# Differential attention: one VectorE combination per query tile, copies and epsilon term on ScalarE, third buffers for queries and gates

## The chip, the core and the metric

The kernel runs on one core of a Trainium2 chip. The metric is the device time of one execution in microseconds. The engines are TensorE (PE in the rows; PEld is its weight load), VectorE (DVE), ScalarE (ACT), GpSimd (POOL) and SyncE (SP), whose queue issues most of the transfers; a name with q at its end (SPq, ACTq) is an engine's own queue of issues and semaphore waits. Each engine works through its instructions in order.

## The reference

The reference is one step of a two-layer hybrid backbone. It is run for 1024 latent tokens and 128 context tokens, width 1024. In each layer an input projection feeds three groups of heads (differential attention, gated DeltaNet, mLSTM); their outputs go through one output projection, and a SwiGLU feed-forward follows. The change touches the attention and, by one buffer, the merging of the two other groups. Cut to these, with names shortened:

```python
# differential attention: 4 heads, two maps m of 64 columns each, values of 128 columns
s = einsum('bqhmd,bkhmd->bhmqk', q, k) * 64 ** -0.5
p = softmax(s, axis=-1)
w = p[:, :, 0] - lam * p[:, :, 1]
a_out = einsum('bhqk,bkhe->bqhe', w, v)
a = rms_norm(a_out, attn_g) * (1 - lam_init)          # over the 128 columns, EPS = 1e-6
# the other two groups
d = rms_norm(o_delta, delta_g) * silu(bg)
m = sigmoid(co) * rms_norm(h_m, mlstm_g)
out = concatenate([a, d, m], -1) @ w_out
```

A latent query reads 1024 latent keys and 128 cached context keys; a context query reads the 128 context keys alone.

## The kernel before

The whole program is unrolled. Everything is float32; matrix products of the projections are made of three passes over a high and a low part (`mm3`). For each layer the order in the source is: `begin` and `w_in` (projections, gates, chunk matrices, inverses), `mixers` (scan, attention, second half of the output projection), the first half of the output projection, the feed-forward.

In `mixers` the scan over chunks (`delta_step`, `mlstm_step`, `merge`) is written first, then the loads of `x`, then the attention, then `w_out`. But the framework is told `schedule_with_timeline_sim=True`: a planner simulates the program with costs of its own and writes the order of each engine's queue. The trace shows attention's instructions between those of the last inverses (`prep2`) and of the scan; in layer 0 they run from 545 to 906 us, in layer 1 from about 2375 to 2757 us. In layer 1 the end of attention runs beside the output projection.

`attention` takes a head at a time, and in it blocks of 256 queries: four latent ones and one of 128 context queries. A block loads its queries (tile `Q`, two buffers, four transfers on the sync queue, line 1235). Then, for each tile of 128 queries (`j`), so 32 latent and 4 context tiles a layer:

1. For both maps, scores of 9 key blocks in three groups of 384 columns (line 1250, PSUM tile `s`, two buffers). VectorE scales each group into `e` (four buffers) and takes the maximum (line 1251); line 1253 takes the maximum of the three; ScalarE makes the exponentials of all 1152 columns in one instruction, with their sum (line 1256).
2. `rz` is the factor of the second map, -lam times the ratio of the sums (lines 1260 and 1261). The weights are not divided by the sum; the norm that follows takes it out again.
3. The combination `e0 + rz * e1`: for groups 0 and 1 (`DVG`) one VectorE instruction each (line 1266), for group 2 two GpSimd instructions (lines 1268 and 1269).
4. Transposes of the combined weights by TensorE, a group into one PSUM tile `t` (one buffer, line 1277), and a copy into `wt` (line 1280): groups 0 and 1 on ScalarE, group 2 (`DVT`) on VectorE. In context tiles the single group 0 goes by the first of each choice.
5. The product with the values (line 1284, PSUM tile `o`). ScalarE squares and sums it (line 1287). VectorE makes the epsilon term, EPS times the square of the first map's sum (line 1289), and adds the mean square (line 1290). GpSimd raises it to the power -0.5 (line 1291), ScalarE scales the product by it (line 1292).

After a block, `out` transposes its tiles (line 1215), scales them (line 1217) and stores them to `CAT` (line 1218). `tail` and `TAIL` could put this off by a block; `TAIL` is False, so they do nothing.

`merge` loads a chunk's gates (tile `bc`, two buffers, line 1184), norms the chunk's rows of the two other groups, multiplies with the gates, transposes and stores to `CAT` (line 1205). Its gate tile is written in place (line 1196) and read last by GpSimd (line 1197).

The names `DVG`, `DVT` and `TAIL` are constants: `(0, 1)`, `(2,)` and `False`.

Of the kernel before, what the change touches and what calls it, by code (L numbers as in the profile page):

```python
# [10 lines left out]
F32R = mybir.dt.float32r  # L11
AF = mybir.ActivationFunctionType
ALU = mybir.AluOpType
# [4 lines left out]
P = 128  # L18
# [12 lines left out]
NCH = 9  # L31
CVW = 1160
CVO = 1156
DVG = (0, 1)
DVT = (2,)
TAIL = False
WTB = 6
PLO = ()
PST = (1, 3, 5, 6)
# [31 lines left out]
class Kern:  # L71
# [1108 lines left out]
    def merge(self, l, c):  # L1180

        nc, S, sc, pz = self.nc, self.S, self.sc, self.pz
        bc = self.t(sc, [P, 512], "bc", 2)
        nc.sync.dma_start(bc, S["BC"][c])
        th = self.t(sc, [P, 512], "bh", 2)
        nc.scalar.activation(th, bc, AF.Tanh, scale=0.5)
        hv = lambda a: a.rearrange("p (h v) -> p h v", v=64)
        src = self.OH[:, c, :]
        r = self.t(sc, [P, 512], "m2", MB)
        nc.scalar.activation(r, src, AF.Square)  # L1190
        ms = self.t(sc, [P, 8], "ms", 2)
        nc.vector.reduce_sum(ms, hv(r), axis=AX.X)
        nc.vector.scalar_tensor_tensor(out=ms, in0=ms, scalar=1.0 / 64, in1=self.me[:, c].rearrange("p a h -> p (a h)"), op0=ALU.mult, op1=ALU.add)
        nc.gpsimd.tensor_tensor(out=ms, in0=ms, in1=self.mhalf[:, :8], op=ALU.pow)
        nc.gpsimd.tensor_tensor(out=hv(r), in0=hv(src), in1=ms[:, :, None].to_broadcast([P, 8, 64]), op=ALU.mult)
        nc.vector.scalar_tensor_tensor(out=bc[:, 0:256], in0=th[:, 0:256], scalar=1.0, in1=bc[:, 0:256], op0=ALU.add, op1=ALU.mult)
        nc.gpsimd.tensor_tensor(out=r[:, 0:256], in0=r[:, 0:256], in1=bc[:, 0:256], op=ALU.mult)
        nc.vector.scalar_tensor_tensor(out=r[:, 256:512], in0=th[:, 256:512], scalar=1.0, in1=r[:, 256:512], op0=ALU.add, op1=ALU.mult)
        pt = self.ps(pz, "z", 2)
        for p in range(4):  # L1200
            nc.tensor.transpose(pt[:, 128 * p:128 * p + 128], r[:, 128 * p:128 * p + 128], self.ident)
        ct = self.t(sc, [P, 4, 128], "m2", MB)
        for i in range(2):
            nc.scalar.activation(ct[:, 2 * i:2 * i + 2], pt[:, 256 * i:256 * i + 256].rearrange("p (a t) -> p a t", a=2), AF.Copy, scale=self.hg[l][:, i:i + 1])
        nc.sync.dma_start(S["CAT"][4:8, :, 128 * c:128 * c + 128].rearrange("a p t -> p a t"), ct)

    def attention(self, l):

        nc, S, at, pa = self.nc, self.S, self.at, self.pa
        tail = []  # L1210

        def out(fin, h, q0, nq):
            pf = self.ps(pa, "o", 2)
# [5 lines left out]
        for h in range(H):  # L1219
            K = []  # L1220
            for m in range(2):
                k = self.t(at, [P, NT + P], "K", 3, F32R)
                r = 64 * (h % 2) + 32 * m
                for lk in range(2):
                    nc.sync.dma_start(k[64 * lk:64 * lk + 64].bitcast(F32), S["KD"][h // 2, lk, r:r + 32].rearrange("r p t -> (r p) t"))
                K.append(k)
            V = self.t(at, [P, 10, 128], "V", 2)
            nc.sync.dma_start(V, S["VD"][:, :, 128 * h:128 * h + 128].rearrange("s p e -> p s e"))
            r0 = 64 * (h % 2)
            for q0 in range(0, NT, 256):  # L1230
                nq = min(256, NT - q0)
                q = self.t(at, [P, 2, 2, 256], "Q", 2, F32R)
                for hh in range(2):
                    for hl in range(2):
                        nc.sync.dma_start(q[64 * hh:64 * hh + 64, :, hl, :nq].bitcast(F32),
                                     S["QD"][h // 2, hl, r0:r0 + 64, :, q0:q0 + nq].rearrange("(m r) p t -> (r p) m t", m=2))
                ctx = q0 >= NL
                kt = [9] if ctx else list(range(9))
                groups = [kt] if ctx else [kt[0:3], kt[3:6], kt[6:9]]
                fin = self.t(at, [P, 256], "fin", 2)  # L1240
                for j in range(nq // 128):
                    es, zs = [], []
                    for m in range(2):
                        e = self.t(at, [P, NT], "e", 4)
                        mx = self.t(at, [P, 4], "mx", 4)
                        for i, ks in enumerate(groups):
                            w = 128 * len(ks)
                            p = self.ps(pa, "s", 2)
                            for hl in range(2):
                                nc.tensor.matmul(p[:, :w], lhsT=q[:, m, hl, 128 * j:128 * j + 128], rhs=K[m][:, 128 * ks[0]:128 * ks[0] + w], start=hl == 0, stop=hl == 1)  # L1250
                            nc.vector.tensor_scalar(out=e[:, GW * i:GW * i + w], in0=p[:, :w], scalar1=0.125, scalar2=None, op0=ALU.mult, op1=ALU.max, accum_out=mx[:, i:i + 1])  # L1251
                        nm = self.t(at, [P, 1], "nm", 4)
                        nc.vector.tensor_reduce(out=nm, in_=mx[:, :len(groups)], axis=AX.X, op=ALU.max, negate=True)
                        z = self.t(at, [P, 1], "zs", 8)
                        ev = e[:, :128 * len(kt)]
                        nc.scalar.activation(ev, ev, AF.Exp, bias=nm, accum_out=z)
                        es.append(e)
                        zs.append(z)
                    rz = self.t(at, [P, 1], "rz", 4)
                    nc.vector.reciprocal(rz, zs[1])  # L1260
                    nc.vector.scalar_tensor_tensor(out=rz, in0=rz, scalar=self.nlam, in1=zs[0], op0=ALU.mult, op1=ALU.mult)
                    for i, ks in enumerate(groups):
                        cs = slice(GW * i, GW * i + 128 * len(ks))
                        w0, w1 = es[0][:, cs], es[1][:, cs]
                        if i in DVG:
                            nc.vector.scalar_tensor_tensor(out=w0, in0=w1, scalar=rz, in1=w0, op0=ALU.mult, op1=ALU.add)
                            continue
                        nc.gpsimd.tensor_scalar(out=w1, in0=w1, scalar1=rz, scalar2=1.0, op0=ALU.mult, op1=ALU.mult)
                        nc.gpsimd.tensor_tensor(out=w0, in0=w0, in1=w1, op=ALU.add)
                    if tail and TAIL:  # L1270
                        out(*tail.pop())
                    WT = []
                    for i, ks in enumerate(groups):
                        n = len(ks)
                        p = self.ps(pa, "t", 1)
                        for a in range(n):
                            nc.tensor.transpose(p[:, 128 * a:128 * a + 128], es[0][:, GW * i + 128 * a:GW * i + 128 * a + 128], self.ident)
                        pv = p[:, :128 * n].rearrange("p (a t) -> p a t", a=n)
                        WT.append(self.t(at, [P, 3, 128], "wt", WTB))
                        (nc.vector.tensor_copy if i in DVT else nc.scalar.copy)(WT[i][:, :n], pv)  # L1280
                    po = self.ps(pa, "o", 2)[:, :128]
                    for i, ks in enumerate(groups):
                        for a, kx in enumerate(ks):
                            nc.tensor.matmul(po, lhsT=WT[i][:, a], rhs=V[:, kx, :], start=kx == kt[0], stop=kx == kt[-1])  # L1284
                    sq = self.t(at, [P, 128], "sq", 2)
                    ms = self.t(at, [P, 1], "ams", 4)
                    nc.scalar.activation(sq, po, AF.Square, accum_out=ms)
                    z2 = self.t(at, [P, 1], "z2", 4)
                    nc.vector.scalar_tensor_tensor(out=z2, in0=zs[0], scalar=EPS, in1=zs[0], op0=ALU.mult, op1=ALU.mult)
                    nc.vector.scalar_tensor_tensor(out=z2, in0=ms, scalar=1.0 / 128, in1=z2, op0=ALU.mult, op1=ALU.add)  # L1290
                    nc.gpsimd.tensor_tensor(out=z2, in0=z2, in1=self.mhalf[:, 0:1], op=ALU.pow)
                    nc.scalar.activation(fin[:, 128 * j:128 * j + 128], po, AF.Copy, scale=z2)
                tail.append((fin, h, q0, nq))
                if not TAIL:
                    out(*tail.pop())
                yield
        if tail:
            out(*tail.pop())


    def w_out(self, l, x, half, pool, tags, psp, bufs, raw):
# [252 lines left out]
```

## Time and profile before

| | |
|---|---|
| runs of the kernel before, median of 3 | 3688.73 us (3680.83 to 3689.36) |
| the profiled execution | 3690.29 us, span 3688.5 us |
| TensorE matmuls | 3517.3 us busy, 95% of the span, 22770 instructions |
| TensorE weight loads | 3345.0 us, 91% |
| VectorE | 2296.8 us, 62%, 5361 instructions |
| ScalarE | 1133.3 us, 31% |
| GpSimd | 662.7 us, 18% |
| mean granted TensorE clock | 0.969 of full speed |

How to read it: times come from one profiled execution; an engine is busy while an instruction runs on it. Matmuls are pipelined and their ends are modelled, so a busy TensorE isn't one at its peak. Shares over the span mix stages with different limits, so the rows below are for stretches. A group of instructions has a line of the kernel, an engine, an operation, the tile written and those read, shapes and a count, and then busy us, the mean ns of one, and the idle time just before them with what ended it. A wait is put down to the release that came last.

### The profile page before, as it was taken

What the parts mean: (1) busy time and instruction counts of PE and PEld (TensorE: products, weight loads), DVE (VectorE), ACT (ScalarE), POOL (GpSimd) and SP (SyncE); (2) the same over time, 40 slices, a digit from 0 to 9 for tenths busy, and PEclk for the clock granted to TensorE, in tenths of its full rate; (3) what the DMA queues carried; (4) which work ended last, traced back from release to release, by engine and by line L of the source; (5) the groups of instructions that cost most, each with busy time, mean ns of one, the idle gap of its engine ahead of it and who ended that gap; (6) DMA issues with size and microseconds to landing.
All of it is one profiled execution on the core that took longest, in us unless ns stands there. A gap on an engine that the chain in (4) does not pass through costs nothing.

```text
span 3688.5 us, 59491 instructions
## 1 busy us (share of the span) xinstructions
PE 3517.3 (95%) x22770; PEld 3345.0 (91%) x22770; DVE 2296.8 (62%) x5361; ACT 1133.3 (31%) x2383; POOL 662.7 (18%) x903
## 2 busy tenths in 40 slices
PE   7999989987999999999999998999899999999998
PEld 6998888986999999999989888888788999999997
DVE  7797778887465556654486478578867243333335
ACT  6324325455241111111143341344545111111111
POOL 2014322474110000000020243035612000000001
PEclk8999988999999999999999999899999999999999
DMA  5477643864222222221132672578341111111111
GB/s 209 137 243 263 222 114 118 269 186 146 66 66 81 78 83 86 97 71 49 56 118 88 223 265 93 143 218 230 106 134 47 41 42 48 43 41 41 46 46 58
DMA packets 279011, 434.14 MB, mean 118 GB/s; under 512 B 26568, under 2 KB 188424, under 8 KB 278472
## 3 DMA queue, kind: packets, MB, share of 16 engines
q1 hardware_dynamic: 249496, 324.30, 27.6%
q10 hardware_dynamic: 29232, 106.05, 8.9%
q8 instruction: 180, 2.95, 0.3%
q14 instruction: 103, 0.84, 0.1%
HBM read 315.85 MB, written 114.39 MB: 117 GB/s over the span
## 4 chain that ended last, share of the span: by engine, by line
PE 78%; DVE 10%; DMA 5%; issue 3%; ACT 2%; POOL 1%; SPq 1%; ACTq 0%; POOLq 0%; DVEq 0%
PE pd L189 7%; PE pd L190 6%; PE pd L191 6%; PE pg L191 5%; PE pu L190 5%; PE pu L191 5%; PE pu L189 5%; PE pg L190 5%; PE pg L189 5%; PE dn L189 5%; PE dn L190 5%; PE dn L191 5%; PE s L1250 3%; PE o L1284 2%; DMA Q<-QD 1%
## 5 line engine op out<-in xcount | busy, mean ns | idle before, releaser
L362 DVE SCALAR_TENSOR_TENSOR x<-pd,mod,x 128x256 f32<-128x256 f32 (+1 forms) x832 | 404.8, 514 | 597.2 <-PE pd L191 596.0
L183 ACT CAST wh<-wr 128x1024 fp32r<-128x1024 f32 (+1 forms) x219 | 229.1, 1047 | 877.7 <-PE pu L190 462.1
L184 DVE TENSOR_TENSOR wl<-wr,wh 128x1024 fp32r<-128x1024 f32 (+1 forms) x219 | 268.7, 1233 | 169.7 <-ACT wh L183 169.2
L299 POOL TENSOR_TENSOR nacc<-nacc,nsq 128x384 f32<-128x384 f32 x48 | 51.8, 1080 | 1755.4 <-issue 1572.5
L189 PE MATMUL pd<-hh,wh 128*128 128x384 f32 x1056 | 359.4, 340 | 7.3 <-DVE x L362 5.1
L189 PE MATMUL pg<-uh,wh 128*128 128x384 f32 x1056 | 357.4, 338 | 2.6 <-ACT uh L342 2.6
L190 PE MATMUL pg<-ul,wh 128*128 128x384 f32 x1056 | 357.8, 339 | 1.0 <-DVE ul L347 1.0
L189 PE MATMUL pu<-uh,wh 128*128 128x384 f32 x1056 | 355.7, 337 | 0.0
L190 PE MATMUL pu<-ul,wh 128*128 128x384 f32 x1056 | 355.5, 337 | 0.0
L190 PE MATMUL pd<-hl,wh 128*128 128x384 f32 x1056 | 355.5, 337 | 0.0
L191 PE MATMUL pg<-uh,wl 128*128 128x384 f32 x1056 | 354.6, 339 | 0.0
L191 PE MATMUL pd<-hh,wl 128*128 128x384 f32 x1056 | 354.4, 337 | 0.0
L191 PE MATMUL pu<-uh,wl 128*128 128x384 f32 x1056 | 350.4, 336 | 0.0
L189 PE MATMUL dn<-uh,wh 128*128 128x384 f32 x864 | 296.6, 343 | 5.7 <-ACT gw L952 4.4
L190 PE MATMUL dn<-ul,wh 128*128 128x384 f32 x864 | 295.9, 342 | 0.0
L191 PE MATMUL dn<-uh,wl 128*128 128x384 f32 x864 | 295.5, 342 | 0.1
L1250 PE MATMUL s<-K,Q 128*128 128x384 f32 (+1 forms) x800 | 223.6, 388 | 30.9 <-DVE e L1251 18.1
L1251 DVE TENSOR_SCALAR_CACHE_REDUCE e<-s 128x384 f32<-128x384 f32 (+1 forms) x400 | 208.9, 540 | 33.6 <-PE s L1250 27.1
L189 PEld LDWEIGHTS pd<-hh,wh 128*128 128x128 f32 x1056 | 198.8, 188 | 18.6 <-issue 7.7
L189 PEld LDWEIGHTS pg<-uh,wh 128*128 128x128 f32 x1056 | 199.6, 189 | 4.5 <-ACT uh L342 2.8
L385 DVE TENSOR_TENSOR hs<-pu,hs 128x384 f32<-128x384 f32 x132 | 73.1, 554 | 208.5 <-PE pu L191 201.7
L191 PEld LDWEIGHTS pg<-uh,wl 128*128 128x128 f32 x1056 | 199.1, 189 | 3.8
(354 smaller groups left out, 8233.1 us busy)
## 6 DMA issues: line engine op xcount, KB each, us to landing
wr<-in_w_gu_dram ACTq DMA_DIRECT2D x88, 512.0 KB
aw<-in_w_mod_dram SPq DMA_DIRECT2D x96, 256.0 KB
wr<-in_w_dn_dram ACTq DMA_DIRECT2D x44, 512.0 KB
wr<-in_w_st_dram ACTq DMA_DIRECT2D x36, 512.0 KB
rd<-RD SPq DMA_DIRECT2D x36, 512.0 KB
aw<-in_w_mod_dram SPq DMA_DIRECT2D x32, 512.0 KB
Q<-QD SPq DMA_DIRECT2D x128, 128.0 KB
RM<-em SPq DMA_DIRECT2D x36, 384.0 KB
```

What stands on the lines that cost most here:

```text
L183: nc.scalar.copy(hi, r)
L184: (eng or nc.vector).tensor_tensor(out=lo, in0=r, in1=hi.bitcast(F32), op=ALU.subtract)
L189: mm(out, lhsT=wh, rhs=xh, start=start, stop=False)
L190: mm(out, lhsT=wh, rhs=xl, start=False, stop=False)
L191: mm(out, lhsT=wl, rhs=xh, start=False, stop=stop)
L299: (nc.gpsimd if k in PST else nc.vector).tensor_tensor(out=self.acc[g], in0=self.acc[g], in1=s, op=ALU.add)
L362: nc.vector.scalar_tensor_tensor(out=x[g][k][:, lo:hi], in0=ps[:, lo:hi], scalar=gate[:, k, cnd:cnd + 1], in1=x[g][k][:, lo:hi], op0=ALU.m ...
L385: nc.vector.tensor_mul(s, pu[:, :GW], s)
L1250: nc.tensor.matmul(p[:, :w], lhsT=q[:, m, hl, 128 * j:128 * j + 128], rhs=K[m][:, 128 * ks[0]:128 * ks[0] + w], start=hl == 0, stop=hl == 1)
L1251: nc.vector.tensor_scalar(out=e[:, GW * i:GW * i + w], in0=p[:, :w], scalar1=0.125, scalar2=None, op0=ALU.mult, op1=ALU.max, accum_out=mx[ ...
L1284: nc.tensor.matmul(po, lhsT=WT[i][:, a], rhs=V[:, kx, :], start=kx == kt[0], stop=kx == kt[-1])
```

## The change

In each latent query tile, the combination becomes one VectorE instruction over all 1152 columns; the two GpSimd instructions go. All copies out of the `t` tile are on ScalarE. The epsilon term is made by two ScalarE activations: a square with the scale sqrt(EPS), and an identity with the scale 1/128 and the first as its bias. The tile `Q` gets a third buffer, and so does `merge`'s tile `bc`. The constants and the unused `tail` go with them. In context tiles (128 columns) the combination stays what it was.

```diff
-        bc = self.t(sc, [P, 512], "bc", 2)
+        bc = self.t(sc, [P, 512], "bc", 3)
...
-                q = self.t(at, [P, 2, 2, 256], "Q", 2, F32R)
+                q = self.t(at, [P, 2, 2, 256], "Q", 3, F32R)
...
-                    for i, ks in enumerate(groups):
-                        cs = slice(GW * i, GW * i + 128 * len(ks))
-                        w0, w1 = es[0][:, cs], es[1][:, cs]
-                        if i in DVG:
-                            nc.vector.scalar_tensor_tensor(out=w0, in0=w1, scalar=rz, in1=w0, op0=ALU.mult, op1=ALU.add)
-                            continue
-                        nc.gpsimd.tensor_scalar(out=w1, in0=w1, scalar1=rz, scalar2=1.0, op0=ALU.mult, op1=ALU.mult)
-                        nc.gpsimd.tensor_tensor(out=w0, in0=w0, in1=w1, op=ALU.add)
-                    if tail and TAIL:
-                        out(*tail.pop())
+                    w0, w1 = [e[:, :128 * len(kt)] for e in es]
+                    nc.vector.scalar_tensor_tensor(out=w0, in0=w1, scalar=rz, in1=w0, op0=ALU.mult, op1=ALU.add)
...
-                        (nc.vector.tensor_copy if i in DVT else nc.scalar.copy)(WT[i][:, :n], pv)
+                        nc.scalar.copy(WT[i][:, :n], pv)
...
-                    nc.vector.scalar_tensor_tensor(out=z2, in0=zs[0], scalar=EPS, in1=zs[0], op0=ALU.mult, op1=ALU.mult)
-                    nc.vector.scalar_tensor_tensor(out=z2, in0=ms, scalar=1.0 / 128, in1=z2, op0=ALU.mult, op1=ALU.add)
+                    nc.scalar.activation(z2, zs[0], AF.Square, scale=math.sqrt(EPS))
+                    nc.scalar.activation(z2, ms, AF.Identity, scale=1.0 / 128, bias=z2)
...
-                tail.append((fin, h, q0, nq))
-                if not TAIL:
-                    out(*tail.pop())
+                out(fin, h, q0, nq)
```

## Rows read from the trace of the kernel before

**Rows 1.** busy time by stretch: us of each engine in brackets' order, granted clock, DMA

```profile
545.00:905.00 360.00, 328.62 (x2734) 294.06 (x2735) 296.63 (x990) 195.26 (x470) 169.99 (x211) 0.94 0.62 185
2375.00:2760.00 385.00, 354.11 (x2615) 325.96 (x2613) 305.40 (x986) 190.63 (x446) 167.64 (x212) 0.94 0.59 172
1200.00:1400.00 200.00, 199.90 (x1145) 197.61 (x1144) 119.72 (x261) 30.77 (x47) 0.00 (x0) 1.00 0.25 82
```

**Rows 2.** waits of TensorE, 545 to 905 us: total us, times, longest

```profile
PE s L1250 <- DVE e L1251: 7.8, 15, 1.1
PE t L1277 <- ACT wt L1280: 6.6, 9, 2.7
PE s L1250 <- DMA Q<-QD: 5.1, 4, 1.9
PE o L1284 <- DVE wt L1280: 4.5, 6, 1.3
```

**Rows 3.** the same, 2375 to 2760 us

```profile
PE s L1250 <- DVE e L1251: 10.3, 17, 1.5
PE s L1250 <- DMA Q<-QD: 5.0, 2, 3.1
PE o L1284 <- DVE wt L1280: 3.1, 3, 2.2
```

**Rows 4.** groups by line and shape, ScalarE, whole span

```profile
L1256 ACT ACTIVATE e<-e,nm 128x1152 f32<-128x1152 f32 x128 | 161.0, 1257 | 88.8 <-DVE nm L1253 85.0 <-DVE z L1290 2.5 <-DVE den L1171 0.5
L1280 ACT COPY wt<-t 128x384 f32<-128x384 f32 x128 | 60.7, 474 | 31.4 <-PE t L1277 31.2
L861 ACT COPY X<-Nd 32x128 f32<-32x128 f32 x136 | 40.2, 295 | 81.4 <-DMA RD<-X 50.8 <-DVE Nd L839 29.0
L154 ACT ACTIVATE ea<-par 128x8 f32<-128x8 f32 x2 | 0.3, 200 | 0.0
```

**Rows 5.** score matmuls: their group, 545 to 905 us; their line, whole span

```profile
L1250 PE MATMUL s<-K,Q 128*128 128x384 f32 (+1 forms) x400 | 112.0, 388 | 13.4 <-DVE e L1251 7.8 <-DMA Q<-QD 5.1
...
L1250 PE MATMUL s<-K,Q x800: 222/339/689, 545.4 to 2727.2; 128*128 128x384 f32 x160
```

**Rows 6.** groups by line and shape, VectorE, whole span

```profile
L1266 DVE SCALAR_TENSOR_TENSOR e<-e,rz,e 128x384 f32<-128x384 f32 x128 | 105.4, 862 | 1.0
L724 DVE SCALAR_TENSOR_TENSOR cv<-cv,cwh,cv 128x1156 f32<-128x1156 f32 x48 | 68.2, 1420 | 0.7
```

**Rows 7.** groups of GpSimd, 545 to 905 us

```profile
L1269 POOL TENSOR_TENSOR e<-e,e 128x384 f32<-128x384 f32 x32 | 36.0, 1126 | 1.8
L1268 POOL TENSOR_SCALAR e<-e,rz 128x384 f32<-128x384 f32 x32 | 26.4, 826 | 142.9 <-DVE rz L1261 104.1 <-PE s L1250 9.2 <-PE o L1284 5.9
```

**Rows 8.** timelines, VectorE and GpSimd: start us, us, instruction

```profile
588.27 1.13 DVE L1266 SCALAR_TENSOR_TENSOR e<-e,rz,e 128x384 f32<-128x384 f32 x2
...
588.22 1.64 POOL L1268 TENSOR_SCALAR e<-e,rz 128x384 f32<-128x384 f32 x1 [3.81 <-ACT T L864]
...
598.82 0.59 POOL L1268 TENSOR_SCALAR e<-e,rz 128x384 f32<-128x384 f32 x1 [4.88 <-PE px L893]
```

**Rows 9.** groups of VectorE, 545 to 905 us

```profile
L1280 DVE COPY wt<-t 128x384 f32<-128x384 f32 x32 | 17.6, 549 | 3.1 <-PE t L1277 2.9
L1289 DVE SCALAR_TENSOR_TENSOR z<-zs 128x1 f32<-128x1 f32 x36 | 9.2, 256 | 3.7 <-ACT e L1256 3.6
L1290 DVE SCALAR_TENSOR_TENSOR z<-ams,z 128x1 f32<-128x1 f32 x36 | 8.7, 241 | 5.8 <-ACT sq L1287 5.5
```

**Rows 10.** waits of the sync queue, 545 to 905 us

```profile
SPq L1184 <- POOL m L1197: 20.3, 5, 7.4
SPq L1235 <- PE s L1250: 19.3, 7, 10.7
```

**Rows 11.** query loads, whole span: ns min/median/max

```profile
L1235 SPq DMA_DIRECT2D Q<-QD x160: 573/599/1730, 534.3 to 2700.3; - x160
```

**Rows 12.** waits of VectorE, 545 to 905 us

```profile
DVE e L1251 <- PE s L1250: 13.0, 19, 2.9
```

More of the change, by code (lines that the diff above doesn't have):

```diff
@@ L33 @@
 CVO = 1156
-DVG = (0, 1)
-DVT = (2,)
-TAIL = False
 WTB = 6
@@ L1209, in attention @@
         nc, S, at, pa = self.nc, self.S, self.at, self.pa
-        tail = []
         def out(fin, h, q0, nq):
@@ L1288, in attention @@
                     z2 = self.t(at, [P, 1], "z2", 4)
-                    nc.vector.scalar_tensor_tensor(out=z2, in0=zs[0], scalar=EPS, in1=zs[0], op0=ALU.mult, op1=ALU.mult)
-                    nc.vector.scalar_tensor_tensor(out=z2, in0=ms, scalar=1.0 / 128, in1=z2, op0=ALU.mult, op1=ALU.add)
+                    nc.scalar.activation(z2, zs[0], AF.Square, scale=math.sqrt(EPS))
+                    nc.scalar.activation(z2, ms, AF.Identity, scale=1.0 / 128, bias=z2)
                     nc.gpsimd.tensor_tensor(out=z2, in0=z2, in1=self.mhalf[:, 0:1], op=ALU.pow)
                     nc.scalar.activation(fin[:, 128 * j:128 * j + 128], po, AF.Copy, scale=z2)
-                tail.append((fin, h, q0, nq))
-                if not TAIL:
-                    out(*tail.pop())
+                out(fin, h, q0, nq)
                 yield
-        if tail:
-            out(*tail.pop())
     def w_out(self, l, x, half, pool, tags, psp, bufs, raw):
```

## The prediction, made before the change was run

> **What bounds the kernel now.** I read the stretches first, because a share over the whole span would mix stages. The two attention stages are 545 to 905 us (layer 0) and about 2375 to 2760 us (layer 1); attention, the last part of the inverse and the scan run together there. In them the tensor engine's matmuls are busy 328.6 of 360 us and 354.1 of 385 us, VectorE 296.6 and 305.4, ScalarE 195.3 and 190.6, GpSimd 170.0 and 167.6; in the feed-forward stretch from 1200 us TensorE is busy 199.9 of 200 us, and nothing that the change touches runs [rows 1]. So the change can only pay in some 745 us of the span, and the prize there, if TensorE's work stays as it is, is its idle time: 31.4 + 30.9 = 62.3 us, plus what is stretched inside its busy time.
>
> Next I read the waits of TensorE in these stages. The reader is to see that no single releaser is large: score matmuls wait for VectorE to empty their PSUM buffer (7.8 and 10.3 us), for the query transfer (5.1 and 5.0), the value matmuls for the copy that VectorE makes (4.5 and 3.1), the transposes for the copies that ScalarE makes (6.6 in layer 0) [rows 2, 3]. Three of the four go back to VectorE or the query load. A second sign that VectorE is what the others wait for: the latent tiles' exponentials on ScalarE sat 85.0 us, over both layers, until VectorE delivered the row maximum [rows 4]. The score matmuls also last longer than they need: median 339 ns over all 800, mean 388 over the 400 of layer 0 [rows 5].
>
> TensorE's weight loads, the second number of each stretch, are busy 294.1 of 360 and 326.0 of 385 us, in layer 0 a little less than VectorE [rows 1]; whether TensorE is full or not is therefore open, and the first rival turns on it. The Trainium skill (Perfetto Trace Analysis, Identifying the Most-Contended Engine) holds that for TensorE the weight loads' busy share is the measure and the matmuls' is not.
>
> **The change part by part.** A layer has 36 tiles of 128 queries: 32 latent ones with 9 key blocks in three groups, and 4 context ones with one group.
>
> *The combination.* VectorE now does groups 0 and 1 in two instructions of 384 columns. Their mean is 862 ns [rows 6], so 1.72 us per latent tile, 64 x 0.862 = 55.2 us per layer. GpSimd does group 2: 26.4 + 36.0 = 62.4 us per layer [rows 7], all of which goes. In their place comes one instruction of 1152 columns. The trace has the same operation at 1156 columns in the convolution: 1.42 us [rows 6]. That is the lower bound. The upper bound is three pieces at today's mean, 2.59 us. Which end is nearer depends on why the pieces take 862 ns. One pair took 1.13 us for both, while GpSimd's multiply, issued 0.05 us before it, took 1.64 us against 0.59 us when it met no pair [rows 8]: the two engines exclude each other on these operands. So 1.72 - 1.13 = 0.59 us of a pair is waiting, 0.30 per instruction. After the change one instruction instead of two can be held up, and GpSimd's work in the stage falls from 170.0 to 107.6 us: 0.30 x 0.63 = 0.19. I take 1.42 + 0.19 = 1.61 us, 51.5 us per layer. The value is nearer the lower end since the row at 1156 columns is the same operation.
>
> The Trainium skill (SBUF — State Buffer, Who interferes with whom) says the same as a rule: a VectorE instruction with two SBUF inputs and a GpSimd one that reads SBUF hold a shared port pair exclusively, and the later one is blocked to the end. The rule also speaks against the change: a hold of 1.4 us at a stretch is longer for the scan's GpSimd instructions than two holds of 0.57. By it the total hold per tile still falls, from 1.13 plus GpSimd's own two to 1.42, so the sum would be the same.
>
> *The third copy* (128 x 384 out of PSUM) leaves VectorE, 32 x 0.55 = 17.6 us per layer [rows 9], and costs ScalarE 32 x 0.474 = 15.2 us [rows 4].
>
> *The epsilon term.* Two one-column instructions leave VectorE, 9.2 + 8.7 = 17.9 us per layer [rows 9], and come on ScalarE. The nearest rows there are 200 ns for 8 columns and 295 ns for a small copy; I take 0.20, 36 x 0.40 = 14.4 us (21.2 at the other end) [rows 4]. The square sum is made on ScalarE too, so one hand-over to VectorE goes from the chain before the power on GpSimd.
>
> *Sum for the engines, per layer.* VectorE: 51.5 - 55.2 - 17.6 - 17.9 = -39.2 us of 296.6 (13%); with the bounds of the new instruction -45.3 (32 x 1.42) to -7.8 (32 x 2.59). Even the dear end is a saving. ScalarE: +29.6, to 225 of 360 us, still below VectorE's 257; what hides it is ScalarE's idle 165 us. GpSimd: -62.4. TensorE's work: none.
>
> *The third buffers.* They add no instruction. The sync queue, which issues all these loads in order, stood 20.3 us in layer 0 before gate loads until GpSimd had freed a gate buffer, and 19.3 us before query loads until score matmuls had freed a query buffer, the largest of several such entries [rows 10]. What is queued behind is the scan's inputs and the outputs. With a third buffer the four loads of a query block can go one block sooner, past the loads of the scan behind which the planner would otherwise put them; at 0.6 us of issue each (160 issues in all) [rows 11] they delay those loads by 2.4 us once per block, which the scan's own double buffers cover; if not, it is 20 x 2.4 = 48 us of queue per layer, of which only what a matmul waits for counts. I take the query wait of TensorE (10.1 us over both layers) as gone, and the gate buffer at nothing: no matmul row waits for it, and the ScalarE operation that does is in the scan's last step, beside attention work. A loss by a load that now comes later isn't excluded; I carry 10 us to either side for both buffers.
>
> *What reaches the end.* TensorE's waits: VectorE's copy, 4.5 + 3.1 = 7.6, goes entirely; the query load, 10.1, goes; of the waits for the emptied score buffer, 18.1, I take half, 9, since VectorE loses 13% of its work and not its queue. Together 26.7 us. Of the stretch inside score matmuls, (388 - 339) x 400 = 19.6 us per layer, half again: 20 over both layers. What is late next is the transposes' wait for ScalarE, taken as unchanged. Sum: 47 us. The profiled execution took 3690.3 us (span 3688.5 and 1.8 around it; the median of the runs is 3688.7), so 3690 - 47 = **3643 us**, 1.3% faster.
>
> **Rivals.**
>
> *The stage follows VectorE entirely* (0.15). If TensorE is loaded as its weight loads show, 294.1 of 360 us [rows 1], it has room for what VectorE saves, and the stage shrinks by VectorE's share: 360 x 39.2/296.6 + 385 x 39.2/305.4 = 48 + 49 = 97 us, 3593 us. For it: ScalarE's 85 us of waits for VectorE. Against it: the scan's serial chain and the loads at the end of the stage don't shrink with VectorE. The page on trace analysis named above would have it so.
>
> *It doesn't do what it says* (0.15). TensorE is busy over 91% of both stages; the work is put in order by a planner whose own costs the trace does not show, and the time that VectorE gains is spent waiting for TensorE instead. Then only the copy's wait and part of the query wait go, about 10 us: 3680 us, not to be told from before. For it: VectorE already waits 13.0 us of layer 0 for score matmuls [rows 12].
>
> *ScalarE's queue takes the wait over* (0.12, slower). The transposes have one PSUM buffer: the next group can't be written before the copy of the last is done. All three copies now stand in ScalarE's queue, where an exponential of 1.26 us [rows 4] may be ahead; the combination, moreover, must be complete before the first group can start. If each of the 64 third copies sat out one exponential, TensorE would lose 64 x 1.26 = 81 us against 47 gained: 3724 us; at three in four, 61 lost, 3704. It decides from 47/64 = 0.73 us per tile. Against it: today the waits for ScalarE's copies are 6.6 us for 64 copies of layer 0, those for VectorE's 4.5 us for 32 [rows 2], so ScalarE is the quicker of the two.
>
> **The numbers.** My forecast has 0.58; its own range is 3612 (VectorE's 39 us saved in full in both layers) to 3663 (the stretch doesn't go). The range for 8 in 10 runs from 3598 to 3695: it leaves out about half of the first rival and most of the last. Faster by over 0.3%, which is 11 us and about what a measurement of this kernel can tell from no change, is 0.73 (the forecast and the first rival); within it 0.15; slower 0.12.
>
> **What would show it.** The new instruction at 1.4 to 1.8 us, VectorE busy about 39 us less per stage, GpSimd some 62 less, ScalarE some 30 more; score matmuls nearer 339 ns; no score matmul waiting for a query load; the two stages together shorter by 40 to 60 us and every stretch outside them unchanged. It is wrong if the new instruction is near 2.6 us, if transposes wait for ScalarE's copies by over 0.7 us a tile, or if the stages keep their length while VectorE's busy share drops.

## The result, and the profile after

| | median of the runs (lowest to highest, number) |
|---|---|
| before | 3688.24 us (3680.83 to 3689.36, 4) |
| after | 3656.09 us (3653.01 to 3664.35, 4) |
| after / before | 0.9919, 95% interval 0.9901 to 0.9937 |

The change made the kernel faster by 0.8%, about 30 us: a gain of the kind and in the place that was forecast, inside the forecast's own range of 3612 to 3663 us and 13 us above its 3643.

The first lines of the page of the kernel after; behind each engine its busy us, share of the span and instructions:

```profile
span 3651.2 us, 59023 instructions
...
PE 3496.0 (96%) x22770; PEld 3337.4 (91%) x22770; DVE 2230.3 (61%) x5089; ACT 1183.9 (32%) x2591; POOL 553.1 (15%) x775
```

The profiled span went from 3688.5 to 3651.2 us, 37.3 less; that is more than 30 because the profiled execution of the kernel after is the fastest of its four, and that of the kernel before (3690.3 us) is slower than its median. To find where, cut it at the first score matmul of each layer and at the start of the output projection (the first matmul of its second pass, 0.4 to 2.3 us behind the very first). Busy time by stretch has, per row, the stretch, its us, the busy us and instructions of PE, PEld, DVE, ACT and POOL, the granted clock, the DMA share and GB/s. The two attention stages of the kernel before, cut this way:

```profile
545.40:904.80 359.40, 328.42 (x2733) 293.89 (x2733) 296.48 (x989) 194.86 (x469) 169.99 (x211) 0.94 0.62 185
...
2373.40:2700.80 327.40, 297.30 (x2257) 269.33 (x2257) 268.13 (x891) 168.91 (x396) 158.89 (x201) 0.93 0.66 192
```

The same view of the kernel after:

```profile
544.50:886.50 342.00, 318.29 (x2704) 290.17 (x2705) 263.26 (x855) 216.98 (x561) 112.25 (x145) 0.95 0.66 195
...
2354.70:2666.70 312.00, 288.11 (x2248) 264.52 (x2249) 238.23 (x771) 191.31 (x488) 110.55 (x143) 0.94 0.70 202
```

The stages are 17.4 and 15.4 us shorter, 32.8 of the 37.3. The rest of the span, before, between and behind them, gave 4.5 us together. VectorE lost 33.2 and 29.9 us in them, GpSimd 57.7 and 48.3; ScalarE gained 22.1 and 22.4. TensorE's idle time fell from 31.0 to 23.7 and from 30.1 to 23.9 us, which is 13.5 us; its busy time fell by 10.1 and 9.2, and some of that is work that no longer falls between the cuts (29 and 9 matmuls fewer).

Waits of TensorE in the kernel after, 545 to 905 us (total us, times, longest), to be read against [rows 2]:

```profile
PE t L1265 <- ACT wt L1268: 7.9, 5, 3.9
PE y L1136 <- DMA rm<-RM: 5.4, 3, 2.5
PE s L1246 <- DVE e L1247: 3.2, 10, 0.5
...
PE s L1246 <- DMA Q<-QD: 1.0, 1, 1.0
...
PE t L1265 <- DVE e L1259: 0.8, 1, 0.8
```

The same, 2354 to 2792 us, against [rows 3]:

```profile
PE s L1246 <- DMA Q<-QD: 5.8, 2, 3.0
PE t L1265 <- ACT wt L1268: 5.4, 6, 2.3
PE s L1246 <- DVE e L1247: 4.0, 5, 2.9
...
PE t L1265 <- DVE e L1259: 3.5, 5, 1.1
PE y L1136 <- DMA rm<-RM: 3.4, 1, 3.4
```

[rows 3] begin at 2375 us, behind the first score matmul of layer 1, and so leave out its wait. From the timeline of TensorE and, for the load `rm`, from the waits of 545 to 905 us, kernel before:

```profile
2373.36 1.01 PE L1250 MATMUL s<-K,Q 128*128 128x384 f32 x2 [2.02 <-DMA Q<-QD]
```

```profile
PE y L1139 <- DMA rm<-RM: 1.1, 1, 1.1
```

Four things are to be seen. The waits of the value matmuls for VectorE's copy have gone. Those of the score matmuls for their buffer fell from 18.1 to 7.2 us over both layers, more than forecast; those for the query load from 12.1 (the 10.1 of the prediction and these 2.0) to 6.8, less than forecast, with 5.8 of what is left in layer 1. Two came up on the transposes: ScalarE's copies, 13.3 us, of which 6.9 were there before ([rows 2] and 0.3 us in layer 1), and the combination, 4.3, of which 1.1 were there. And one came up in the scan: its matmuls wait 8.8 us for the load `rm` on the sync queue, 1.1 before. TensorE's waits for loads of every kind in the two stages are 18.0 us, against 14.8 before: they moved from the queries to the scan, and didn't shrink.

The groups of the changed instructions in the kernel after, by line and shape, whole span:

```profile
L1252 ACT ACTIVATE e<-e,nm 128x1152 f32<-128x1152 f32 x128 | 160.9, 1257 | 43.2 <-DVE nm L1249 42.5
...
L1259 DVE SCALAR_TENSOR_TENSOR e<-e,rz,e 128x1152 f32<-128x1152 f32 x64 | 93.5, 1461 | 1.4
...
L1268 ACT COPY wt<-t 128x384 f32<-128x384 f32 x192 | 90.8, 473 | 60.5 <-PE t L1265 60.1
...
L1278 ACT ACTIVATE z<-ams,z 128x1 f32<-128x1 f32 x72 | 21.2, 295 | 1.2
...
L1277 ACT ACTIVATE z<-zs 128x1 f32<-128x1 f32 x72 | 14.7, 205 | 0.4
```

One combination takes 1461 ns, where VectorE's two pieces took 862 each [rows 6] and GpSimd made the third; its median is 1418, near the 1420 ns of the convolution's row. The exponentials wait 42.5 us for VectorE's row maximum, half of the 85.0 of [rows 4].

VectorE's largest wait, 545 to 905 us, kernel after:

```profile
DVE e L1247 <- PE s L1246: 33.8, 36, 3.8
```

It was 13.0 us [rows 12]: of the 33 us that VectorE was relieved of in layer 0, it spends 21 waiting for TensorE. What a further us of relief would be worth can't be read from this wait; the run `dve_load` below measures an added one.

The sync queue, same stretch, kernel after:

```profile
SPq L1231 <- PE s L1246: 14.3, 4, 7.6
SPq L1231 <- PE t L1265: 11.1, 2, 7.8
...
SPq L1181 <- POOL m L1194: 4.7, 3, 3.8
```

It stands 25.4 us for query buffers in the first two rows, 23.4 in the same two before; over all its releasers line 1231 stands 41.2 us, against 58.1 before. For gate buffers it stands 15.6 us less [rows 10]. Both fell by about the same, so which of the two buffers mattered can't be read from that; the experiments tell them apart.

### The profile page after: what moved, and what is told of

Same layout as the page of the kernel before. It is cut to its first block, busy times and chain, and to the rows that moved or that the text cites. A ratio compares the mean times of both kernels' runs of the same rounds, so it can differ in the third digit from the quotient of the medians.

```text
span 3651.2 us, 59023 instructions
## 1 busy us (share of the span) xinstructions
PE 3496.0 (96%) x22770; PEld 3337.4 (91%) x22770; DVE 2230.3 (61%) x5089; ACT 1183.9 (32%) x2591; POOL 553.1 (15%) x775
## 3 DMA queue, kind: packets, MB, share of 16 engines
q8 instruction: 180, 2.95, 0.3%
## 4 chain that ended last, share of the span: by engine, by line
PE 83%; DVE 7%; DMA 4%; issue 2%; ACT 2%; POOL 1%; SPq 0%; POOLq 0%; ACTq 0%; DVEq 0%
PE pd L186 7%; PE pd L188 6%; PE pd L187 6%; PE pg L188 5%; PE pu L187 5%; PE pu L188 5%; PE pu L186 5%; PE pg L187 5%; PE dn L186 5%; PE pg L186 5%; PE dn L188 5%; PE dn L187 5%; PE s L1246 3%; PE o L1272 3%; PE t L1265 1%
## 5 line engine op out<-in xcount | busy, mean ns | idle before, releaser
L187 PEld LDWEIGHTS pg<-ul,wh 128*128 128x128 f32 x1056 | 199.2, 189 | 3.3 <-DVE ul L344 2.2
```

What stands on the lines that cost most here:

```text
L187: mm(out, lhsT=wh, rhs=xl, start=False, stop=False)
```

## The experiments

The ratio is to the kernel before, run on the same chip in the same job, since that kernel's own median moved from 3688 to 3693 us between jobs. The us lost or gained between two variants are the difference of their ratios times 3690. The question is which part of the change made the 30 us: VectorE's relief, GpSimd's departure from the shared operands, or the buffers; and whether ScalarE's new work was free.

**Undo one part at a time.** The combination in pieces, with GpSimd's third:

```diff
-                    w0, w1 = [e[:, :128 * len(kt)] for e in es]
-                    nc.vector.scalar_tensor_tensor(out=w0, in0=w1, scalar=rz, in1=w0, op0=ALU.mult, op1=ALU.add)
+                    for i, ks in enumerate(groups):
+                        cs = slice(GW * i, GW * i + 128 * len(ks))
+                        w0, w1 = es[0][:, cs], es[1][:, cs]
+                        if i < 2:
+                            nc.vector.scalar_tensor_tensor(out=w0, in0=w1, scalar=rz, in1=w0, op0=ALU.mult, op1=ALU.add)
+                            continue
+                        nc.gpsimd.tensor_scalar(out=w1, in0=w1, scalar1=rz, scalar2=1.0, op0=ALU.mult, op1=ALU.mult)
+                        nc.gpsimd.tensor_tensor(out=w0, in0=w0, in1=w1, op=ALU.add)
```

> The changed kernel with the combination alone put back: two VectorE pieces of 384 columns and group 2 on GpSimd. VectorE theory (about half of each us that VectorE is spared in the attention stages reaches the end, 32 of 66): VectorE has 12 us more (105 against 94), so about 6 us slower than the changed kernel, near 3662 us; the pieces last 0.8 to 0.9 us again. Buffer theory (the gain is the earlier query and gate loads): no difference, 3656. Exclusion theory (the gain is GpSimd out of VectorE's way, for the scan as well): most of the gain is lost, 3675 or more.

3664.95 us (3663.34 to 3668.79), ratio 0.9932 (0.9920 to 0.9944). Most of the gain is still there with GpSimd back at its pieces and VectorE's at 837 ns, so the two engines' exclusion is not what the change lives on.

The third copy back on VectorE:

```diff
-                        nc.scalar.copy(WT[i][:, :n], pv)
+                        (nc.vector.tensor_copy if i == 2 else nc.scalar.copy)(WT[i][:, :n], pv)
```

> The changed kernel with the third copy alone put back on VectorE. VectorE theory: 35 us more on VectorE, about 16 us slower than the changed kernel, near 3672. Buffer and exclusion theories: no difference, 3656. If ScalarE's queue costs something now, it gets faster: the transposes' waits for ScalarE's copies (12 us over both layers after the change) fall and the time is under 3650.

3670.44 us (3662.93 to 3680.28), ratio 0.9944 (0.9928 to 0.9960): about 9 us lost against the change.

The epsilon term back on VectorE:

```diff
-                    nc.scalar.activation(z2, zs[0], AF.Square, scale=math.sqrt(EPS))
-                    nc.scalar.activation(z2, ms, AF.Identity, scale=1.0 / 128, bias=z2)
+                    nc.vector.scalar_tensor_tensor(out=z2, in0=zs[0], scalar=EPS, in1=zs[0], op0=ALU.mult, op1=ALU.mult)
+                    nc.vector.scalar_tensor_tensor(out=z2, in0=ms, scalar=1.0 / 128, in1=z2, op0=ALU.mult, op1=ALU.add)
```

> The changed kernel with the epsilon term alone put back on VectorE. VectorE theory: 36 us more on VectorE, about 16 us slower than the changed kernel, near 3672. Buffer and exclusion theories: no difference, 3656.

3650.04 us (3646.97 to 3658.85), ratio 0.9893 (0.9878 to 0.9908). No loss; by the ratios 10 us less than the change, though the intervals overlap.

Both tiles back at two buffers, all engine work as in the change:

```diff
-        bc = self.t(sc, [P, 512], "bc", 3)
+        bc = self.t(sc, [P, 512], "bc", 2)
...
-                q = self.t(at, [P, 2, 2, 256], "Q", 3, F32R)
+                q = self.t(at, [P, 2, 2, 256], "Q", 2, F32R)
```

> The changed kernel with two buffers for queries and for gates. VectorE theory: the score matmuls' wait for query loads comes back to 10 us, so 5 us slower at most, 3656 to 3662. Buffer theory: most of the gain is lost, 3675 or more.

3691.72 us (3684.45 to 3707.19, 11 runs), ratio 1.0009 (0.9995 to 1.0024). The whole gain is gone, though VectorE is relieved as in the change. (The profiled execution of this variant took 3706.7 us, 15 above its median, so its trace shows more waits than a typical one.) This is the largest effect of any single part, and the prediction had put 10 us of 47 on it.

**The buffers alone, and which of the two.** The kernel before with three buffers for `Q` and for `bc` (the opposite of the last diff), and with three for `Q` alone:

> The kernel before with the two third buffers alone. Undoing the buffers took the whole gain away, so two theories are left. Buffers alone (the query and gate loads held the stages, VectorE did not): this gives the whole gain, near 3656 us. Both needed (the loads come in time only with the third buffer, but then VectorE's own work is what the stages wait for, so that each part alone gives little): 3670 to 3688.

> The kernel before with a third query buffer alone. Query buffer alone theory: near 3660. Both needed: 3675 to 3688, no difference that can be told.

3685.64 us (3680.80 to 3697.27), ratio 0.9992 (0.9980 to 1.0005), and 3686.21 us (3679.54 to 3694.17), ratio 0.9988 (0.9977 to 0.9998): 0.1% at most. In the first of them the query waits of TensorE are down to 3.3 us over both layers, but its waits for VectorE to empty the score buffer stay at 11.0 and 10.3 us. As measured, the buffers are worth next to nothing without the relief, and the relief nothing without the buffers.

The two runs don't show that VectorE is what the buffers alone run into. In `only_q` the score matmuls wait 18.8 us for VectorE over both layers, as before (18.1), and hardly at all for queries. The score matmuls of layer 0 in the kernel before and in `only_q` (shortest, median and longest ns, first and last start in us):

```profile
L1250 PE MATMUL s<-K,Q x400: 227/339/689, 545.4 to 891.0; 128*128 128x384 f32 x128, 128*128 128x128 f32 x6
```

```profile
L1246 PE MATMUL s<-K,Q x400: 221/339/690, 544.8 to 879.4; 128*128 128x384 f32 x128, 128*128 128x128 f32 x6
```

They are done 11.6 us sooner, as soon as in the change (880.1). Then TensorE stands at the end of the stage; its waits from 885 to 915 us, `only_q`:

```profile
PE pd L186 <- ACT ch L1302: 13.4, 1, 13.4
PE o L1211 <- ACT fin L1286: 8.3, 3, 6.4
```

The first is for the inputs of the output projection, which starts at 911 us for 904. So part of what the buffer may give alone is lost there. Why those inputs come late, and whether another order of the planner's would bring them sooner, no run shows.

The change with two buffers for `Q` (three for `bc`), and with two for `bc` (three for `Q`), each one line of the last diff:

> The changed kernel with two query buffers, gates at three. If the query buffer carries it: 3680 to 3692, with score matmuls waiting some 10 us a layer for query loads. If the gate buffer carries it: 3656.

> The changed kernel with two gate buffers, queries at three. If the query buffer carries it: 3656, within 5 us. If the gate buffer carries it (the sync queue stands before gate loads, and the scan's loads behind it come late): 3680 to 3692.

3682.61 us (3679.16 to 3692.80), ratio 0.9985 (0.9972 to 0.9998), and 3662.25 us (3657.64 to 3673.19), ratio 0.9924 (0.9907 to 0.9942). The query buffer carries it; the gate buffer can't be told from nothing, as the prediction had it. Nor does the sync queue's standing for gates follow the buffers: in layer 0 it was 17.8 us in `back_q` with three and 13.7 in `back_bc` with two.

Waits of TensorE with two query buffers and the rest as in the change (`back_q`), 545 to 905 us:

```profile
PE s L1246 <- DMA Q<-QD: 11.0, 3, 4.2
PE t L1265 <- ACT wt L1268: 5.0, 5, 1.6
PE s L1246 <- DVE e L1247: 2.2, 7, 0.6
```

The relief empties score buffers sooner (2.2 us against 7.8 of [rows 2]), the score matmuls come to the next query block sooner, and there they wait for its load: 11.0 us here and 12.4 in layer 1, 23.4 against 12.1 before and 6.8 after. That is 17 us more than in the change, but the 8.8 us for `rm` aren't there in `back_q`, so waits for loads of every kind differ by 5 (23.4 against 18.0). The two attention stages of `back_q`, cut as above:

```profile
544.30:908.70 364.40, 335.23 (x2729) 303.35 (x2730) 260.64 (x851) 217.27 (x562) 112.11 (x146) 0.92 0.61 183
2376.20:2689.90 313.70, 281.18 (x2201) 259.88 (x2202) 228.91 (x743) 185.56 (x467) 108.22 (x141) 0.92 0.69 200
```

They are 24 us longer than in the change, as much as the runs lost (0.9985 - 0.9919 = 0.0066 of 3690). Of this, 14 are idle time of TensorE and 10 are busy time, at a granted clock of 0.92 for 0.95 and 0.94. How a wait can lengthen the busy time is seen at the first query wait of layer 0, near 630 us; its row in the timeline of TensorE, `back_q`:

```profile
633.36 0.69 PE L1246 MATMUL s<-K,Q 128*128 128x384 f32 x1 [2.95 <-DMA Q<-QD]
```

and busy time by stretch around it, `back_q` (granted clock third from the right):

```profile
625.00:630.00 5.00, 4.54 (x70) 4.11 (x65) 4.13 (x14) 3.73 (x13) 0.08 (x1) 1.00 0.80 218
630.00:635.00 5.00, 2.05 (x16) 1.42 (x17) 1.33 (x6) 0.75 (x2) 1.40 (x3) 0.76 1.00 259
635.00:640.00 5.00, 5.00 (x28) 4.32 (x26) 1.89 (x6) 0.48 (x1) 0.00 (x0) 0.50 0.31 78
640.00:645.00 5.00, 5.00 (x31) 4.48 (x30) 1.56 (x5) 1.47 (x2) 0.88 (x2) 0.50 0.42 148
```

The same stretches of the kernel after, where no load is waited for:

```profile
630.00:635.00 5.00, 5.00 (x47) 4.15 (x45) 3.46 (x12) 2.01 (x5) 0.00 (x0) 1.00 1.05 231
635.00:640.00 5.00, 4.51 (x25) 3.25 (x24) 4.12 (x18) 3.36 (x8) 1.99 (x5) 1.00 0.82 250
640.00:645.00 5.00, 4.20 (x30) 3.63 (x30) 4.61 (x15) 4.63 (x14) 1.10 (x3) 1.00 0.51 163
```

After a wait of 2.95 us, `back_q` ran 10 us at a granted clock of 0.50, the lower of the two levels, with TensorE shown as busy all the while; the kernel after stayed at 1.00. In the kernel before, a wait of 1.5 us at about the same place was followed by 0.51 in the stretch 630 to 635. Such a wait is dearer than its own length. Not every one is: the kernel after, a query wait in layer 1 and the 10 us behind it:

```profile
2446.69 0.58 PE L1246 MATMUL s<-K,Q 128*128 128x384 f32 x2 [3.00 <-DMA Q<-QD]
```

```profile
2446.70:2456.70 10.00, 10.00 (x85) 10.00 (x85) 8.36 (x26) 4.39 (x9) 2.79 (x4) 1.00 0.92 258
```

**How much is an us of VectorE or ScalarE worth now?** The change with one more instruction per latent tile, on a tile of zeros that nothing else reads, on VectorE and then on ScalarE:

```diff
+        jk = at.tile([P, 1152], F32, name=self.nm("jk"))
+        nc.gpsimd.memset(jk, 0.0)
...
+                    if not ctx:
+                        nc.vector.scalar_tensor_tensor(out=jk, in0=jk, scalar=rz, in1=jk, op0=ALU.mult, op1=ALU.add)
```

```diff
+                    if not ctx:
+                        nc.scalar.activation(jk, jk, AF.Copy, scale=rz)
```

> The changed kernel with one more VectorE instruction per latent tile, of the combination's kind and width on a tile of zeros that nothing else reads: about 64 x 1.45 = 93 us more on VectorE. If VectorE's time still holds the stages with the buffers in place, half or more of it reaches the end: 3700 us or more. If the stages now wait for loads or TensorE, little of it does: under 3680.

> The changed kernel with one more ScalarE copy of 1152 columns per latent tile, on a tile of zeros that nothing else reads: about 64 x 1.2 = 77 us more on ScalarE. Prediction's view (ScalarE's idle time hides what it gets): within 10 us of 3656. If ScalarE's queue has become a limit, as the epsilon term suggests, whose way back to VectorE saved 6 us: 3680 us or more, some 0.4 us for each us.

The added groups, first in the kernel with more VectorE work and then in that with more ScalarE work, by line and shape, whole span:

```profile
L1263 DVE SCALAR_TENSOR_TENSOR jk<-jk,rz 128x1152 f32<-128x1152 f32 x64 | 96.3, 1505 | 0.0
```

```profile
L1263 ACT ACTIVATE jk<-jk,rz 128x1152 f32<-128x1152 f32 x64 | 80.3, 1255 | 18.3 <-DVE rz L1259 14.1 <-DVE e L1249 3.5
```

VectorE's: 3716.0 us (3712.23 to 3727.64), ratio 1.0062 (1.0048 to 1.0076). Against the change's ratio that is 0.0143 of 3690, 53 us for 96.3 us of work, 0.55 us per us. ScalarE's: 3683.25 us (3676.89 to 3689.21), ratio 0.9974 (0.9963 to 0.9986): 20 us for 80.3 us, 0.25 per us. 0.55 is between a stage that VectorE sets us for us and one that TensorE fills. VectorE's price isn't of its own time alone: GpSimd's busy time rose by 25 us in that run (578.0 against 553.1). The Trainium skill (Perfetto Trace Analysis, Identifying the Most-Contended Engine) takes the weight loads' busy share, not the matmuls', as the measure of TensorE's headroom. By it TensorE had room, 290.2 of 342.0 us in layer 0 after the change, but was still busier than VectorE with 263.3; no run decides between these readings.

**One buffer more, and a second look at the epsilon term.** The change with `Q` at four buffers, and the same with the epsilon term on VectorE:

> The changed kernel with a fourth query buffer. If the load of queries still holds the stages: 3645 or less. If three buffers are enough (score matmuls wait 1 us in layer 0 and 6 us in layer 1 for query loads): 3650 to 3660.

> The changed kernel with the epsilon term back on VectorE and a fourth query buffer, as the version that might be best. With the epsilon term back alone it took 3650; if the fourth buffer adds nothing: 3645 to 3655; if query loads still hold layer 1: near 3640.

3656.34 us (3649.73 to 3660.66), ratio 0.9901 (0.9887 to 0.9916): three are enough. And 3667.77 us (3663.63 to 3671.57), ratio 0.9934 (0.9921 to 0.9946). The second is slower than either of its neighbours. It differs from `back_eps`, 0.9893, by a query buffer that should only admit loads sooner, and is 0.4%, 15 us, slower. What differs besides is the order that the planner makes: of VectorE's 5233 instructions, 563 have to be left out before the two traces show the same order, by line and operation. Between the change and `q4`, the same edit, it is 22 of 5089, and the times agree. That the order costs the 15 us is argued from these two pairs, not shown. But a variant of this kernel can be a new order too, and an effect below some 15 us isn't proof of the part that was edited.

## Why the prediction was right, and where its sum was off

*The bound and the place* held. 32.8 of 37.3 us came out of the two attention stages, and the rest of the span kept its length within 4.5 us. Of the signs that were named, the new instruction's time came; the two stages got shorter by 33 us where 40 to 60 was named; VectorE was busy 33 and 30 us less per stage for 39, GpSimd 58 and 48 less for 62, ScalarE 22 more for 30; score matmuls of layer 0 went to 382 ns where "nearer 339" was named, and 6.8 us of query waits stayed.

*The combination* was sized at 1.61 us between 1.42 and 2.59; it took 1.46. Its mean is 0.04 us above its median and above the convolution's row, so waiting for GpSimd adds about that on average and not the 0.19 that was reckoned. *The copy* cost ScalarE 0.473 us as forecast. *The epsilon term* was taken at 2 x 0.20 us; the square took 205 ns, but the identity with a column as its bias 295, so 36 us over both layers and not 29. By groups VectorE lost 12 + 35 + 36 = 83 us against 78 forecast; by its busy line, which counts overlapping records once, 66.5. ScalarE gained 50.6 us by that line against 59, GpSimd lost 109.6 against 125.

*What reaches the end* was forecast at 47 us, 27 of waits and 20 of stretch; the profiled span fell by 37. The wait for the copy went (7.6) and the score buffer's fell by 10.9 (forecast 9). Three steps were mis-sized. First, "What is late next is the transposes' wait for ScalarE, taken as unchanged": it rose by 6.4 us, and the wait for the combination by 3.2. Second, the query wait, "10.1, goes", which was 12.1 with the start of layer 1, fell by 5.3 only, as layer 1 still waits 5.8 us. Third, the delay of the scan's loads, "which the scan's own double buffers cover", wasn't covered: matmuls wait 7.7 us more for `rm`. That the earlier query loads are what delays `rm` is not shown, though in `back_q` no such wait is left. With all this TensorE's idle time fell by 13.5 us. The 20 us of stretch came out near its size but not where it was looked for: TensorE's busy time between the cuts fell by 19 us, but the score matmuls of layer 0 went from a mean of 388 to 382 ns only, 2.4 us of it; the others are spread over all its lines, with the granted clock at 0.95 for 0.94 and 0.94 for 0.93.

*"What hides it is ScalarE's idle 165 us"* wasn't borne out. At the 0.25 us per us that `act_load` measured, the 66 us by groups that ScalarE took on (30 of copies, 36 of the epsilon term) cost 16. At VectorE's 0.55, the 83 us that it lost are worth 46. The difference, 29 us, agrees with the 30 of the runs. By the engines' busy lines, with 88.8 and 67.2 us of added work, the prices are 0.59 and 0.30 and the difference is 24 us. Both prices are measured at the changed kernel with its three query buffers, and each may carry the 15 us of a new order, which is most of ScalarE's 20; so the agreement is rough.

*The buffers as a term of their own* is where the model was wrong, though the total was not. The prediction added 10.1 us for the query buffer to 37 for the relief. As measured, the two don't add up: relief without the query buffer between a loss of 0.1% and a gain of 0.15% (`back_bufs`, `back_q`), buffers without relief 0.1% (`only_bufs`, `only_q`), both together 0.8%. For the relief alone the rows show what takes over: 23.4 us of query waits in `back_q`, and 10 us at half clock behind one of them. The step that was missed is the question what a faster VectorE runs into, which the prediction asked for the transposes and not for the loads. For the buffers alone they don't show it, as the end of layer 0 in `only_q` may hide what they give. That the sum came near the result is thus partly luck: it added two terms that paid only together, and left out what ScalarE's work costs.

*The rivals.* That the stage follows VectorE entirely, 97 us, fell: 0.55 of it. That VectorE's time is spent waiting for TensorE is partly so, 33.8 us in layer 0 against 13.0, and is the whole outcome with two query buffers: `back_bufs` shows 48.7 us of it in its layer 0 (545 to 917 us) and a ratio of 1.0009. That ScalarE's queue takes the wait over exists as a mechanism, at 13.3 us / 64 = 0.21 us per tile, against 0.73 from which it would have decided.

*Open:* which part of the relief pays. The three parts undone one at a time cost 5, 9 and -10 us against the change, all three together (`only_bufs`) 27; by the two prices it would be 6.5, 12 and 10.5, together 29. No run undid two of them. Open too is whether the epsilon term on ScalarE gains or loses. Having it there cost 10 us with three query buffers (0.9893 against 0.9919) and gained 12 with four (0.9934 against 0.9901), both within what an order does. The copy's 9 us and the combination's 5 (0.9932 against 0.9919) are no surer. No version ran clearly faster than the change: `back_eps` has the lowest median, 3650.0, with an interval that overlaps the change's.

## What to carry to other kernels

Where a matmul waits in turn for an engine and for a load, price the relief of the one with the other left as it is, then both: here each alone was worth 0.15% at most and both 0.8%. Count a wait's neighbours too: the query loads' wait shrank and that of the scan's loads grew. Price an engine's us by adding an idle instruction to it and timing that, not by its idle share: VectorE, 77% busy in the stage, was worth 0.55 us per us, and ScalarE, 63% busy, 0.25. Where a planner orders the instructions, find out first how far an edit that should do nothing moves the time (up to 15 us here), and claim no part below that.

## What the runs showed of the hardware

The price of a wait in the granted clock: 2.95 us without a matmul at 630 us, then 10 us at 0.50; but 3.00 us without one at 2447 us, then 10 us at 1.00. Added up over the 36 slices of 20 us from each layer's first score matmul, as (1 - granted clock) x 20 us, TensorE missed 45.0 us before, 38.2 after, 55.0 in `back_q` and 65.6 in `back_bufs`; the profiled times of these are 3690.3, 3653.0, 3685.8 and 3706.7 us. From after to `back_q` that is 17 of 33 us. The sum includes slices in which TensorE had nothing to do, so it is an upper estimate of the clock's part, and it doesn't order the kernels by itself: `only_q` missed 33.2 us and took 3686.2.

On ScalarE the square of one column costs 205 ns, and the identity whose bias is a column, which the instruction ahead of it has just written, 295 ns; whether the bias or the hand-over makes the difference isn't shown. On VectorE the same two steps took 256 and 241 ns on average [rows 9], with a median of 155 each over the whole span. So the two instructions themselves are no shorter on ScalarE; what the saved hand-over is worth isn't measured.
